# Storing a softmax's row reciprocals straight from their columns, one element at a time

## The chip, the cores and the metric

One core of one Trainium2 chip runs the whole program. The metric is the device time of one execution in microseconds (us), as the median of several runs.

## The reference

A decoder block on one sequence of 1024 tokens and 1024 channels, in float32. After a root-mean-square norm, one matrix product gives queries, keys and values for 8 attention heads of 64 channels, the two halves of a spatial gate, and one forget value per head and token. What matters here is the attention:

```python
c = jnp.cumsum(log_f, axis=1)
logits = jnp.einsum('bqhd,bkhd->bhqk', qi, k) * scale + ci[..., None] - c_k
p = jax.nn.softmax(jnp.where(causal, logits, -jnp.inf), axis=-1)
out = jnp.einsum('bhqk,bkhd->bqhd', p, v)
```

The attention's result and the gate's result are joined, multiplied by `w_out` and added to the input. A gated MLP with a short causal convolution and a last norm follow.

## The kernel before, in words

The stages are: input norm and products (to about 205 us in the profile), attention (to about 370), output product and second norm (to about 420), the MLP's up products (to about 840), the down products. Matrix operands are split into a high and a low part, and each product takes three matrix multiplications, so that float32 accuracy is kept. The attention stage is the one that the change touches.

**One head.** Head `h` has 8 blocks of 128 queries. `logits_mm` (L900) multiplies queries and keys into PSUM, block 7 first; `logits_min` (L910) masks on VectorE and finds each row's minimum; `logits_exp` (L927) takes the exponential on ScalarE in place and adds each row into column `j` of `rows[h]`, a tile of 128 rows by 8 blocks. `turn_p` (L935) turns blocks of the exponentials on TensorE (L946), ScalarE copies the high part (L947) and VectorE forms the low part (L948). `values` (L953) multiplies them with the values (L965) into a 64-by-1024 result `attF[p][.., 0, ..]`, with the 64 channels on partitions, two heads to a pair `p`. The result is not normalised there.

**The steps.** A head is five steps; 40 steps are walked by the loop at L1051. A step first turns what the next step needs, then multiplies its own values, and beside that starts the logits of head `h+1`. At step 1 of a head VectorE takes the reciprocals of its row sums (L1075), and `row_tail(h)` (L863) is called. It must bring the reciprocals, which lie as 128 partitions by 8 columns, into the order of the 1024 tokens, and repeat them on 64 partitions: the tile is turned on TensorE to 8 by 128 (L868), copied to SBUF by ScalarE (L869), stored to a 4 KB scratch `rsd[h]` in HBM by a DMA that ScalarE's queue issues (L870), and loaded back, repeated 64 times, into the second half of `attF[p]` by a DMA on SyncE's queue (L871), 256 KB.

**Who uses it.** `pair_half` (L874) multiplies result and reciprocals and splits the product. For pairs 0 to 2 it does so on GpSimd (L880 to L882), two halves of a pair, after its second head; for pair 3 on VectorE and ScalarE at the stage's end. GpSimd has other work in line behind it: in head 2 the low parts of the second half of the gate's output weights (`sg_split`, L716, its line L161), which the filler products need (below), and from head 5 on the attention's output weights (`wo_load`, L1003). The tile of `attF` is one of four buffers of the tag `H`, which the exponentials of odd heads use as well.

**Fillers.** Between the steps TensorE does pieces of another product, the gate's part of the output (`sg_out`, L978, matrix multiplications L990 to L992): one token block of 512 channels each, at steps 1 and 4 of heads 1 to 5, more in head 0. Each needs a load of the input `raw` (L986) on SyncE's queue, is added to it on VectorE (L993), and is stored (L994). `raw` tiles come from four buffers. `head_loads(h+2)` (L809, L813 to L821) brings queries and keys of a later head, about 1.3 MB, once a head.

**What sets the order.** A recording layer places the instructions of each engine in one line; engines run theirs in order and meet at semaphores. SyncE's queue too is one line: a DMA that waits holds up all DMAs behind it. DMAs take one of eight completion semaphores in turn, so a DMA also waits until the one eight places before it has landed. Matrix multiplications and turns of this stage are chained by `seq` (L696), so that their order on TensorE is fixed by the program. Elsewhere, at L391, the program stores 128-by-8 row scales into an 8-by-128 scratch `rbd` in HBM with the same kind of access pattern, once, and loads them back repeated (L392):

```python
act.dma_start(out=rbd.rearrange("a p -> p a"), in_=rstd1)
sp.dma_start(out=rb, in_=rbd.rearrange("a b -> (a b)").unsqueeze(0).to_broadcast((P, 1024)))
```

In the profile L391 shows under the line of a recording helper, L44.

Of the kernel before, what the change touches and what calls it, by code (L numbers as in the profile page):

```python
# [14 lines left out]
P = 128  # L15
# [44 lines left out]
def after(tc, later, earlier):  # L60
    tc.add_manual_dep(later.ins, earlier.ins.name, mybir.DependencyInfo(
        mybir.DependencyClass.NoSync, mybir.DependencyReason.DATA), reason="order")
# [3 lines left out]
def block_kernel(ctx: ExitStack, tc: tile.TileContext, xT, xtok, wuv, wv0, wv1, wqk, cpk, bfv,  # L66
                 ggain, g2r, gfr, wsp, woa, wos, wup, wdn, out):
    nc = tc.nc
    act, dve, pool, pe, sp = Line(nc.scalar, tc), Line(nc.vector, tc), Line(nc.gpsimd, tc), nc.tensor, nc.sync
# [13 lines left out]
    def nm(s):  # L83
        uid[0] += 1
        return f"{s}_{uid[0]}"
# [6 lines left out]
    def sb(tag, shape, dt=F32):  # L92
        return (raws if tag == "raw" else late if tag in LATE else early).tile(shape, dt, tag=tag, bufs=BUFS[tag], name=nm(tag))

    def bank():
        return psa.tile([P, 512], F32, tag="b", bufs=BB, name=nm("pb"))
# [28 lines left out]
    ident = cst.tile([P, P], F32, name="ident")  # L125
# [23 lines left out]
    rsd = drm.tile([8, 8, P], F32, name="rsd")  # L149
# [546 lines left out]
    def seq(m):  # L696

        if order:
            after(tc, m, order[0])
        order[:] = [m]  # L700
# [78 lines left out]
    idr = sb("t01", [P, 1024])  # L779
# [83 lines left out]
    def row_tail(h):  # L863

        p, hh, rs = h // 2, h % 2, rows[h]
        ptr = bank()
        rt = idr[0:8, 640 + P * hh:640 + P * (hh + 1)]
        seq(pe.transpose(ptr[0:8, 0:P], rs, ident))  # L868
        act.copy(rt, ptr[0:8, 0:P])  # L869
        act.dma_start(out=rsd[h], in_=rt)  # L870
        sp.dma_start(out=attF[p][hh * 64:hh * 64 + 64, 1, :],  # L871
                     in_=rsd[h].rearrange("a b -> (a b)").unsqueeze(0).to_broadcast((64, 1024)))

# [177 lines left out]
    for n, step in enumerate(STEPS):  # L1051
        h, s = n // 5, n % 5
# [24 lines left out]
        for c, (g, pt, js) in enumerate(zip(step, now, NEXT[s])):  # L1077
            out_copy = values(g, pt) or out_copy
            last_copy = out_copy
            if h < 7:  # L1080
                for j in js:
                    due.append((h + 1, j, logits_min(h + 1, j, logits_mm(h + 1, j, place()))))
            if s == (1 if h < 7 else 2) and c == (h == 7):
                row_tail(h)
# [594 lines left out]
```

## Time and profile before

| What | Value |
|---|---|
| Median of 3 runs | 1058.69 us (1058.6 to 1058.9) |
| The profiled execution, its own time | 1059.72 us |
| Its span in the trace | 1058.0 us |
| TensorE clock granted, mean | 0.999 |
| TensorE busy | 1046.3 us of the span |
| VectorE, ScalarE, GpSimd busy | 884.0, 571.1, 235.8 us |
| Turns of the row reciprocals (L868) | 8, first at 238.3 us, last at 367.0 us |

Times in the trace count from the start of the span. A row of the timeline gives the start, the duration, the engine, the line, the operation and its operands, and in brackets how long the engine had been idle and for whom it waited. "ACTq" and "SPq" are the queues of ScalarE and SyncE, where a DMA's row is the time of its issue and not of its transfer. Rows of windows give the busy time of each engine in a stretch, then the granted clock, the DMA engines' share and the GB/s that they moved. The prediction shows the rows that it uses.

### The profile page before, as it was taken

What the parts mean: (1) busy time and instruction counts of PE and PEld (TensorE: products, weight loads), DVE (VectorE), ACT (ScalarE), POOL (GpSimd) and SP (SyncE); (2) the same over time, 40 slices, a digit from 0 to 9 for tenths busy, and PEclk for the clock granted to TensorE, in tenths of its full rate; (3) what the DMA queues carried; (4) which work ended last, traced back from release to release, by engine and by line L of the source; (5) the groups of instructions that cost most, each with busy time, mean ns of one, the idle gap of its engine ahead of it and who ended that gap; (6) DMA issues with size and microseconds to landing.
All of it is one profiled execution on the core that took longest, in us unless ns stands there. A gap on an engine that the chain in (4) does not pass through costs nothing.

```text
span 1058.0 us, 14612 instructions
## 1 busy us (share of the span) xinstructions
PE 1046.3 (99%) x5156; PEld 880.3 (83%) x5156; DVE 884.0 (84%) x1297; ACT 571.1 (54%) x1013; POOL 235.8 (22%) x177
## 2 busy tenths in 40 slices
PE   9999999999999999999999999999999999999997
PEld 6988888988889888888888888888888888888885
DVE  6999787777778869998999989989897866897774
ACT  6776544456766746654444444444444544454653
POOL 0003241420420740154333323323321000000000
PEclk9999999999999999999999999999999999999999
DMA  9623466856555344222255322331322899333432
GB/s 323 219 8 134 129 162 167 224 153 190 168 163 170 122 174 173 72 89 100 80 170 179 120 96 94 120 122 59 132 96 80 302 328 314 102 99 100 146 119 94
DMA packets 67184, 155.78 MB, mean 147 GB/s; under 512 B 9028, under 2 KB 9748, under 8 KB 67112
## 3 DMA queue, kind: packets, MB, share of 16 engines
q1 hardware_dynamic: 65800, 154.82, 45.8%
q8 instruction: 40, 0.66, 0.3%
q14 instruction: 32, 0.26, 0.1%
q10 hardware_dynamic: 1312, 0.04, 0.1%
HBM read 111.96 MB, written 42.87 MB: 146 GB/s over the span
## 4 chain that ended last, share of the span: by engine, by line
PE 94%; DVE 2%; DMA 1%; ACT 1%; POOL 1%; issue 0%; SPq 0%; POOLq 0%; ACTq 0%; DVEq 0%
PE k L1529 20%; PE qc L1271 11%; PE qa L1271 11%; PE qd L1271 11%; PE ps L259 5%; PE qb L1271 5%; PE pb L259 5%; PE pb L965 3%; PE pb L946 3%; PE qa L417 2%; PE qc L417 2%; PE qd L417 2%; PE pl L906 2%; PE pl L907 2%; PE pf L990 1%; PE pf L992 1%
## 5 line engine op out<-in xcount | busy, mean ns | idle before, releaser
L1529 PE MATMUL k<-whb,wha 128*128 128x512 f32 x924 | 209.7, 389 | 0.0
L1529 PEld LDWEIGHTS k<-whb,wha 128*128 128x128 f32 x924 | 173.4, 188 | 36.2 <-DVE wha L161 0.2
L1271 PE MATMUL qc<-xT,whb 128*128 128x512 f32 x540 | 129.8, 389 | 0.2 <-ACT whb L155 0.2
L1271 PE MATMUL qa<-xB,wha 128*128 128x512 f32 x528 | 127.5, 390 | 0.0
L1271 PEld LDWEIGHTS qc<-xT,whb 128*128 128x128 f32 x540 | 101.3, 188 | 21.5 <-ACT whb L155 0.5
L1271 PEld LDWEIGHTS qa<-xB,wha 128*128 128x128 f32 x528 | 98.8, 188 | 20.9 <-DVE wha L161 0.4
L155 ACT CAST wha<-sg 128x512 fp32r<-128x512 f32 x77 | 47.8, 622 | 96.7 <-PE k L1529 86.4
L155 ACT CAST whb<-sg 128x512 fp32r<-128x512 f32 x82 | 50.5, 618 | 88.0 <-PE qc L1271 67.7
L161 DVE TENSOR_TENSOR wha<-sg,wha 128x512 fp32r<-128x512 f32 x77 | 52.7, 687 | 40.5 <-ACT wha L155 40.4
L947 ACT CAST pt<-pb 128x512 fp32r<-128x512 f32 (+1 forms) x80 | 42.2, 544 | 43.1 <-PE pb L946 34.2
L1271 PE MATMUL qd<-xB,whb 128*128 128x512 f32 x264 | 63.7, 389 | 0.0
L1271 PE MATMUL qd<-xT,whb 128*128 128x512 f32 x264 | 63.7, 389 | 0.0
L1155 POOL TENSOR_TENSOR sg<-raw 128x512 f32<-128x512 f32 x20 | 31.1, 1556 | 139.5 <-DVE whb L161 78.0
L1271 PE MATMUL qb<-xT,whb 128*128 128x512 f32 x252 | 61.0, 389 | 0.0
L161 DVE TENSOR_TENSOR whb<-sg,whb 128x512 fp32r<-128x512 f32 x82 | 57.0, 697 | 4.4 <-ACT whb L155 4.3
L948 DVE TENSOR_TENSOR pt<-pb,pt 128x512 fp32r<-128x512 f32 (+1 forms) x80 | 48.8, 634 | 12.3 <-ACT pt L947 11.0
L1271 PEld LDWEIGHTS qd<-xT,whb 128*128 128x128 f32 x264 | 49.5, 188 | 10.5 <-DVE u L1378 0.3
L1271 PEld LDWEIGHTS qd<-xB,whb 128*128 128x128 f32 x264 | 49.6, 188 | 10.3
L1271 PEld LDWEIGHTS qb<-xT,whb 128*128 128x128 f32 x252 | 47.2, 188 | 10.0 <-DVE whb L161 0.3
L965 PE MATMUL pb<-pt,V 128*128 128x256 f32 x320 | 52.1, 287 | 0.3 <-DVE pt L948 0.2
L1158 POOL TENSOR_TENSOR sg<-sg,raw 128x512 f32<-128x512 f32 x20 | 33.0, 1650 | 63.8 <-DVE whb L161 63.8
L965 PEld LDWEIGHTS pb<-pt,V 128*128 128x128 f32 x320 | 43.8, 190 | 2.6 <-DVE pt L948 0.4
(411 smaller groups left out, 2271.8 us busy)
## 6 DMA issues: line engine op xcount, KB each, us to landing
raw<-wup SPq DMA_DIRECT2D x44, 512.0 KB
sg<-hx SPq DMA_DIRECT2D x77, 256.0 KB
hx<-hs SPq DMA_DIRECT2D x44, 256.0 KB
hx<-ca SPq DMA_DIRECT2D x35, 256.0 KB
xT<-wdn SPq DMA_DIRECT2D x28, 256.0 KB
x<-kd SPq DMA_DIRECT2D x24, 256.0 KB
A<-xtok SPq DMA_DIRECT2D x8, 512.0 KB
raw<-wqk SPq DMA_DIRECT2D x8, 512.0 KB
```

The source lines that it names most:

```text
L155: act.copy(h, src)
L161: return eng.tensor_tensor(out=l, in0=src, in1=f32(h), op=ALU.subtract)
L259: pe.matmul(banks[m], xs(n, xi, k)[:, ms], w[:, wi, :], start=(first and k == 0 and c == 0 and (own or m % 2 == 0)), stop=(k == 3 and c == ...
L417: pe.matmul(ps, w[:, wi, ks], xs(n, xi, k), start=(first and c == 0), stop=(c == 11), skip_group_check=True)
L946: seq(pe.transpose(ptr[:, c:c + P], tj[jj][:, k * P:(k + 1) * P], ident))
L947: casts.append(act.copy(pt[:, 0, 0:w], ptr[:, 0:w]))
L948: los.append(dve.tensor_tensor(out=pt[:, 1, 0:w], in0=ptr[:, 0:w], in1=f32(pt[:, 0, 0:w]), op=ALU.subtract))
L965: seq(pe.matmul(po[0][:, oo:oo + n], lhs, pt[:, s, o:o + n], start=(k == 0 and s == 0), stop=(s == 1 and half)))
L1155: pool.tensor_tensor(out=s[0], in0=a21, in1=a22, op=ALU.add)
L1158: pool.tensor_tensor(out=s[3], in0=s[1], in1=a12, op=ALU.add)
L1271: pe.matmul(ps, w[:, wi, ks], xb[:, xi, k, :], start=(first and n == 0), stop=(n == 11), skip_group_check=True)
L1529: pe.matmul(banks[bk + m], xh[:, xi, ms], wh[:, wi, :], start=(first and p_ == 0 and n == 0), stop=(p_ == NP - 1 and n == 2), skip_group_c ...
```

## The change

For heads 0 to 6, `row_tail` no longer turns the reciprocals on TensorE and copies them. ScalarE's queue issues a DMA that reads the 128-by-8 tile as it lies and writes its elements to the places in `rsd[h]` at which the load L871 reads them. Head 7 keeps the turn, the copy and the store. The load back is the same. All lines below L865 stand 3 lines further down in the changed file; the text names the lines of the kernel before.

```diff
         p, hh, rs = h // 2, h % 2, rows[h]
-        ptr = bank()
-        rt = idr[0:8, 640 + P * hh:640 + P * (hh + 1)]
-        seq(pe.transpose(ptr[0:8, 0:P], rs, ident))
-        act.copy(rt, ptr[0:8, 0:P])
-        act.dma_start(out=rsd[h], in_=rt)
+        if h < 7:
+            act.dma_start(out=rsd[h].rearrange("a p -> p a"), in_=rs)
+        else:
+            ptr = bank()
+            rt = idr[0:8, 640 + P * hh:640 + P * (hh + 1)]
+            seq(pe.transpose(ptr[0:8, 0:P], rs, ident))
+            act.copy(rt, ptr[0:8, 0:P])
+            act.dma_start(out=rsd[h], in_=rt)
         sp.dma_start(out=attF[p][hh * 64:hh * 64 + 64, 1, :],
                      in_=rsd[h].rearrange("a b -> (a b)").unsqueeze(0).to_broadcast((64, 1024)))
```

## The prediction

> **What bounds the kernel now.** First the page: the engines' shares, then the chain that ended last. Then a table of windows over the middle of the attention stage, of which the sum row of 50 windows of 1 us (230 to 280 us) is shown.
>
> ```profile
> span 1058.0 us, 14612 instructions
> PE 1046.3 (99%) x5156; PEld 880.3 (83%) x5156; DVE 884.0 (84%) x1297; ACT 571.1 (54%) x1013; POOL 235.8 (22%) x177
> PE 94%; DVE 2%; DMA 1%; ACT 1%; POOL 1%; issue 0%; SPq 0%; POOLq 0%; ACTq 0%; DVEq 0%
> ...
> sum 50.00, PE 49.74 PEld 44.13 DVE 37.31 ACT 32.72 POOL 11.35; mean PE 0.99 PEld 0.88 DVE 0.75 ACT 0.65 POOL 0.23
> ```
>
> TensorE has work all the time, in the attention stage too (49.74 of 50 us). So only two things can move the end: TensorE work that goes, and a wait of TensorE that is new. All else has cover, and the question is how thick it is.
>
> **What goes.** Seven turns, seven copies. The rows of L868 and L869, from the views by line, and the turn of head 1 between its neighbours in TensorE's timeline:
>
> ```profile
> L868 PE MATMUL pb<-ident,rs x8: 270/272/274, 238.4 to 367.1; 128*8 128x128 f32 x8
> L868 PEldq EVENT_SEMAPHORE  x7: 51/51/51, 256.3 to 366.5; - x7
> L869 ACT COPY t<-pb x8: 237/238/254, 239.4 to 367.4; 8x128 f32<-8x128 f32 x8
> ...
> 257.26 0.27 PE L868 MATMUL pb<-ident,rs 128*8 128x128 f32 x1
> 257.29 0.65 PE L965 MATMUL pb<-pt,V 128*128 128x256 f32 x4
> ```
>
> A turn lasts 0.27 us, but the next matrix multiplication starts 0.03 us behind it: they are pipelined. With its semaphore (0.05 us) I take 0.03 + 0.05 = 0.08 us each, 7 x 0.08 = 0.6 us. The ends are 7 x 0.03 = 0.2 and 7 x 0.27 = 1.9 us; I stand near the lower, since the starts, not the durations, add up on a full engine. The copies, 7 x 0.24 = 1.7 us, are hidden: ScalarE is busy 32.72 of 50 us. Without that cover they would be 1.7 us of gain.
>
> **What is added: the store's own time.** The attention stage never shows such a store, but L391 is one: 128 x 8 elements of 4 bytes into the same kind of scratch, issued on the same queue. Its issue, the issue of the load that waits for it, the waits of SyncE's queue, and windows of 2 us:
>
> ```profile
> 67.83 0.38 ACTq L44 DMA_DIRECT2D rbd<-rstd  x1
> 77.95 0.33 SPq L392 DMA_DIRECT2D t<-rbd  x1
> SPq L392 <- DMA rbd<-rstd: 7.1, 1, 7.1
> SPq L871 <- DMA rsd<-t: 14.1, 6, 3.7
> ...
> 70.00 0.80 SPq L401 DMA_DIRECT2D G<-wv  x2
> 81.10 0.75 POOL L474 TENSOR_TENSOR G<-G 128x264 f32<-128x264 f32 x1 [79.38 <-DMA G<-wv]
> ...
> 70.00:72.00 2.00, 2.00 (x10) 1.65 (x10) 2.00 (x3) 0.62 (x1) 0.00 (x0) 1.00 1.39 15
> 72.00:74.00 2.00, 2.00 (x11) 1.65 (x10) 2.00 (x4) 0.62 (x1) 0.00 (x0) 1.00 0.14 13
> 76.00:78.00 2.00, 2.00 (x11) 1.65 (x10) 2.00 (x4) 2.00 (x5) 0.00 (x0) 1.00 0.75 20
> 82.00:84.00 2.00, 2.00 (x11) 1.65 (x10) 2.00 (x3) 0.09 (x1) 0.75 (x1) 1.00 1.03 401
> ```
>
> From issue to landing 77.95 - 67.83 = 10.1 us, of which SyncE's queue waited 7.1. The rearranged store of today costs that queue 14.1 us in six waits, 2.4 each. And it is not only late: loads issued at 70.00 moved at 13 to 20 GB/s (last column) until the store was done, and the first was usable at 81.10; at 82 the same queue runs at 401. So a store is a **blackout** of about 10 us for all transfers. Seven of them are 70 us in a stage of 155.
>
> The Trainium skill, "DMA: Bandwidth & Descriptors", section "Anatomy of one DMA", fits a transfer's time as about 2.0 us plus its bytes over 436 GB/s, from transfers that GpSimd issued. By it the 4 KB take an estimated 2.0 us, L871 would be issued about as early as today, and the sum would hold the gain alone. The trace's 10.1 us disagrees, which is why this stands below only as a rival.
>
> Under load the store can be shorter by nothing that I see, and longer: at L391 the queue was empty when it was issued. At head 1's store loads are still running (windows of 1 us):
>
> ```profile
> 256.00:257.00 1.00, 1.00 (x9) 0.91 (x8) 0.84 (x4) 0.73 (x2) 0.00 (x0) 1.00 1.04 221
> 257.00:258.00 1.00, 1.00 (x9) 0.91 (x8) 0.83 (x3) 1.00 (x2) 0.00 (x0) 1.00 0.53 107
> ```
>
> 221 + 107 = 328 KB still to move, some 0.9 us at 370 GB/s. I take 10.1 + 0.9 = 11.0 us, with 10 as the lower end and 15 as the upper (half as long again).
>
> **What is moved.** The order of the changed program differs from before on few places, all in this stage. On ScalarE the store stands earlier, between the two casts (L947) that follow the reciprocal, not behind the next exponential. On SyncE L871 moves by one to two places and the filler loads L986 of heads 1 to 4 now stand behind it. Other DMAs keep their order. So what is queued behind the waiting L871 is: filler loads, filler stores, the next `head_loads`, the output weights.
>
> On ScalarE the store's issue (0.38 us) sits ahead of a cast, and in head 2 it waits for the reciprocal (276.01 to 276.21 below) where the cast began at 275.66: 276.21 + 0.38 - 275.66 = 0.9 us late. That cast is used by TensorE a step later, over 3 us; cost nothing, 0.9 us without that cover.
>
> ```profile
> 255.78 0.59 ACT L947 CAST pt<-pb 128x512 fp32r<-128x512 f32 x1 [0.56 <-PE pb L946]
> 275.66 0.59 ACT L947 CAST pt<-pb 128x512 fp32r<-128x512 f32 x1 [0.22 <-PE pb L965]
> 256.04 0.20 DVE L1075 RECIPROCAL rs<-rs 128x8 f32<-128x8 f32 x1
> 276.01 0.20 DVE L1075 RECIPROCAL rs<-rs 128x8 f32<-128x8 f32 x1
> ```
>
> **The waits, head by head.** Stores go out at about 256.4 (head 1: the cast's end, 255.78 + 0.59) and 276.3 (head 2). With 11.0 us L871 goes at 267.4 and 287.3, where it went at 260.48 and 279.15. Its 256 KB then take 2.5 us at least (issued at 260.48, moved by 263 in the windows) and 5.1 at most (head 7: 369.62 to 374.69, with other loads ahead); I take 3.0. The first who could be late:
>
> ```profile
> 260.48 0.45 SPq L871 DMA_DIRECT2D H<-rsd  x1
> 279.15 0.45 SPq L871 DMA_DIRECT2D H<-rsd  x1
> 262.00:263.00 1.00, 1.00 (x9) 0.91 (x8) 0.54 (x2) 0.99 (x2) 0.00 (x0) 1.00 0.92 277
> 369.62 0.45 SPq L871 DMA_DIRECT2D H<-rsd  x1
> 374.69 1.29 DVE L884 TENSOR_TENSOR H<-H 128x512 f32<-128x512 f32 x2 [3.11 <-DMA H<-rsd]
> ...
> 266.86 1.28 POOL L880 TENSOR_TENSOR H<-H 128x512 f32<-128x512 f32 x1 [48.47 <-DVE H L974]
> 272.65 5.05 POOL L161 TENSOR_TENSOR whl<-raw,whl 128x512 fp32r<-128x512 f32 x4
> 279.21 0.39 PE L991 MATMUL pf<-whl,G 128*128 128x512 f32 x1
> 290.59 0.69 DVE L993 TENSOR_TENSOR raw<-pf,raw 128x512 f32<-128x512 f32 x1 [0.84 <-issue]
> ```
>
> *GpSimd, pair 0.* L880 starts at 267.4 + 3.0 = 270.4, not 266.86. Behind it in line stand, unchanged, the rest of the pair and the four low parts of the gate's weights. Today GpSimd also idles 0.5 us in that row; from 270.4 it runs through, and the four end at 280.6, not 277.7. The fourth is needed by TensorE's L991 at 279.21: a **hole of 1.4 us** on the full engine. At a store of 10.1 us it is 0.5, at 12 it is 2.4: it grows one to one.
>
> *Filler loads.* Behind head 2's L871 stands the load for the filler added at 290.59: issued at 287.8, in at about 291.3 (3.5 us, behind L871's bytes). VectorE has about 1.2 us until TensorE feels it, and the hole above moves all of this by 1.4. Nothing, until the store takes some 11.5 us. The one behind head 1's (added at 271.57) has a microsecond more. All others are needed 9 us or more after their new issue.
>
> *`head_loads`, output weights, other pairs.* Needed about 18 us after they can start; the blackout takes 11. GpSimd's pair 2 and weight splits end some 2 us later, at 367, before the output product takes them. Nothing; with a store of 15 us here too little is left.
>
> **The sum.** -0.6 + 1.4 = +0.8 us on the profiled execution's 1059.72 (span 1058.0 and 1.7 around it). The median of the runs is 1.0 below that execution, so +0.8 on 1058.69: **1059.5 us**.
>
> **The rivals.**
>
> *The store is much longer under load: slower.* For it: 13 to 20 GB/s for what shares the engines, and at heads 0 to 3 the queue is not empty. Against: the queue at 70 us was backed up during most of that store as well, and it still took 10.1. The mechanism is the hole of pair 0 with the late filler load of head 2 added. It decides from 11.7 us of store on, where the sum passes +2.1. At 14 us: 1.4 + 3.0 = 4.4 for the hole; the filler load in at 276.3 + 14 + 0.5 + 3.5 = 294.3 against 290.59 + 1.2, 2.5 us; less 0.6: +6.3, **1065.0 us**. At 15 us 1067. The Trainium skill, same page, section "Latency and other measured facts", puts HBM access at 0.2 us on average and 2 us at high load. By that the busier attention stage would lengthen every element's write, this rival's direction; no row here shows such a store under load.
>
> *The store is short: a small gain.* If L391's 10.1 us are its place and not its kind, L871 goes about as today, and only TensorE's gain stays: 1058.69 - 0.6 = **1058.1 us**, at most 1.9 less. For it: the six stores of today land in 2.4 us. Against: these write 8 rows of 512 bytes.
>
> **How the numbers follow.** A difference under 0.2%, 2.1 us, can't be told from no change here. Forecast (store of 10 to 11.7 us) 0.44, all within 0.2%; long store 0.45, slower; short store 0.11, of which 0.03 is over 0.2% faster (more bounded by the turns than their 0.27 us). Faster 0.03, same 0.44 + 0.08 = 0.52, slower 0.45. The likeliest case alone reaches from 1058.1 to 1060.8. The range of eight in ten, from the short store (1058.1, less half a microsecond for how far its gain is known) to one of 15 us: 1057.6 to 1067.
>
> **What would show it.** After: SyncE waits 9 to 11 us before each L871 of heads 0 to 6; GB/s near 20 behind each store; the first L880 near 270 us and a wait of TensorE for L161's weights near 279. Wrong if the waits stay near 2.4 us (short store), or if VectorE waits for `raw` at L993 or TensorE for `head_loads` (long store). A loss spread over all heads would mean that contention, not the one hole, is the price.

## The result, and the profile after

The changed kernel is slower: 1076.98 us in the median (1066.47 to 1080.38, 6 runs) against 1058.86 (1058.60 to 1059.05) for the kernel before on the same chip, ratio 1.0154 with a 95% interval of 1.0127 to 1.0181. The prediction was 1059.5 us, its range 1057.6 to 1067. In four later measurements the unaltered changed kernel gave 1063.7 to 1065.1 us, so two things are to be explained: some 5 to 6.5 us over the kernel before on the same chip that came back each time, and the rest of the first measurement. The profiled execution is the 1066.47 us one, so the traces show the first part and not the second. The text below names lines of the changed file; the rows of dead_late, pool_order and head1_twice bear the line numbers of those files, which differ by a few.

The page of the changed kernel: span, engines, the DMA queue that holds the stores (packets, MB, share of time; before it had 1312 packets), and the shares of the chain that ended last.

```profile
span 1064.7 us, 14585 instructions
PE 1047.6 (98%) x5149; PEld 880.1 (83%) x5149; DVE 885.6 (83%) x1297; ACT 571.1 (54%) x1006; POOL 237.4 (22%) x177
...
q10 hardware_dynamic: 8480, 0.04, 0.5%
...
PE 82%; DVE 7%; DMA 6%; ACT 2%; issue 2%; POOL 1%; SPq 1%; ACTq 0%; POOLq 0%; DVEq 0%
```

The queue has 7168 packets more, 7 x 1024, for the same bytes: one for each element. DMA was 1% of the chain and is 6%. The waits of SyncE's queue and of TensorE (the latter from 205 to 420 us), each with its sum, count and longest:

```profile
SPq L874 <- DMA rsd<-rs: 52.5, 6, 10.8
```

```profile
PE pf L994 <- POOL whl L161: 2.7, 4, 1.9
PE pl L910 <- DMA x<-kd: 1.7, 1, 1.7
PE ps L1219 <- DVE xn L1201: 1.4, 2, 0.8
```

SyncE's wait for the reciprocals has grown from 14.1 to 52.5 us (six waits in both), and TensorE has three waits that the kernel before did not have. Where they lie, the windows show: TensorE is the first number after the comma.

```profile
...
275.00:280.00 5.00, 3.07 (x17) 2.18 (x16) 3.39 (x7) 1.91 (x4) 4.94 (x5) 1.00 1.07 264
280.00:285.00 5.00, 4.28 (x22) 3.08 (x23) 1.25 (x2) 0.80 (x2) 3.85 (x4) 1.00 1.25 71
350.00:355.00 5.00, 3.30 (x22) 2.74 (x21) 2.13 (x6) 2.06 (x8) 0.03 (x1) 1.00 0.97 257
395.00:400.00 5.00, 4.21 (x24) 3.32 (x22) 4.96 (x7) 2.16 (x7) 4.92 (x4) 1.00 0.79 311
400.00:405.00 5.00, 4.34 (x24) 3.35 (x23) 4.80 (x7) 3.85 (x8) 2.40 (x2) 1.00 0.68 211
sum 30.00, PE 24.03 PEld 18.73 DVE 18.93 ACT 15.62 POOL 18.57; mean PE 4.00 PEld 3.12 DVE 3.16 ACT 2.60 POOL 3.10
```

The kernel before, in the same windows:

```profile
sum 30.00, PE 29.98 PEld 25.92 DVE 24.31 ACT 21.47 POOL 13.36; mean PE 5.00 PEld 4.32 DVE 4.05 ACT 3.58 POOL 2.23
```

29.98 - 24.03 = 5.95 us of idle TensorE (the sums hold 270 to 275 us as well), of the 6.7 by which the span grew (1058.0 to 1064.7), in three places and not spread over the heads. The first is the hole that the prediction named. The chain from 250 to 300 us (start, duration, what):

```profile
255.81 12.93 DMA rsd<-rs
268.76 3.51 DMA H<-rsd
272.43 1.29 POOL H L883
273.78 0.62 POOL A L884
...
277.63 4.99 POOL whl L161 x4
282.67 0.50 PE pf L994
```

Head 1's store takes 12.93 us, its load back 3.51, and GpSimd starts pair 0 at 272.43; the gate's weights come behind it and TensorE waits for each. The second hole is new to the prediction. The timeline around head 5's store (issues on ScalarE's and SyncE's queues, and TensorE's wait in brackets):

```profile
335.44 0.41 ACTq L867 DMA_DIRECT2D rsd<-rs  x1
335.47 0.98 SPq L813 DMA_DIRECT2D x<-qd  x1
...
342.21 0.25 SPq L821 DMA_DIRECT2D x<-ncd  x1
349.22 0.44 SPq L874 DMA_DIRECT2D H<-rsd  x1
353.78 0.48 PE L910 MATMUL pl<-x,x 66*128 66x512 f32 x1 [1.70 <-DMA x<-kd]
```

And the last of the same loads before:

```profile
330.60 0.45 SPq L821 DMA_DIRECT2D x<-ncd  x1
```

`head_loads` for head 7, whose last issue was at 330.60, now waits on SyncE's queue until head 4's store is in (L874 at 329.51) and a filler's store behind it (3.2 us more), and so goes out at 335.47 to 342.21, into head 5's store (335.44 to 349.22): both are late. This **piling up** turned out to be the heart of the matter. The third hole, at 395 to 405 us, stands behind the last pair and the second norm.

### The profile page after: what moved, and what is told of

The parts are those of the page before. It is cut to its first block, busy times and chain, and to the rows that moved or that the text cites. A ratio compares the mean times of both kernels' runs of the same rounds, so it can differ in the third digit from the quotient of the medians.

```text
span 1064.7 us, 14585 instructions
## 1 busy us (share of the span) xinstructions
PE 1047.6 (98%) x5149; PEld 880.1 (83%) x5149; DVE 885.6 (83%) x1297; ACT 571.1 (54%) x1006; POOL 237.4 (22%) x177
## 4 chain that ended last, share of the span: by engine, by line
PE 82%; DVE 7%; DMA 6%; ACT 2%; issue 2%; POOL 1%; SPq 1%; ACTq 0%; POOLq 0%; DVEq 0%
PE k L1532 20%; PE qc L1274 11%; PE qa L1274 11%; PE qd L1274 11%; PE qb L1274 5%; PE pb L968 2%; PE qa L417 2%; PE ps L259 2%; PE pb L949 2%; PE qc L417 2%; PE qd L417 2%; DMA x<-kd 1%; PE pl L909 1%; DMA rsd<-rs 1%; PE pl L910 1%
## 5 line engine op out<-in xcount | busy, mean ns | idle before, releaser
L161 DVE TENSOR_TENSOR wha<-sg,wha 128x512 fp32r<-128x512 f32 x77 | 53.0, 690 | 39.7 <-ACT wha L155 39.6
L161 DVE TENSOR_TENSOR whb<-sg,whb 128x512 fp32r<-128x512 f32 x82 | 57.1, 698 | 4.4 <-ACT whb L155 4.3
L1274 PEld LDWEIGHTS qb<-xT,whb 128*128 128x128 f32 x252 | 47.2, 188 | 10.1 <-DVE whb L161 0.3
```

Source lines behind the costliest of these rows:

```text
L161: return eng.tensor_tensor(out=l, in0=src, in1=f32(h), op=ALU.subtract)
L1274: pe.matmul(ps, w[:, wi, ks], xb[:, xi, k, :], start=(first and n == 0), stop=(n == 11), skip_group_check=True)
```

## The experiments

Theories: **W**, the waits: only the late load back counts, by the holes behind it. **B**, the blackout: what the stores do to all other transfers counts, even if nobody waits for the stores. Two more were formed on the way: **P**, piling up: a store is long because loads are under way, and holds back loads that are then under way at the next one. **C**, the clock: a TensorE wait makes the granted clock fall, and costs more than itself. "Store" below is the time from its issue to the issue of the load that needs it. For head 6 this is not the store's length: SyncE's queue stands there for GpSimd and for filler stores, and in the kernel before, too, the load goes 8.4 us after (353.18 to 361.62). So only heads 0 to 5 are counted.

**The changed kernel again.**

> The changed kernel once more, unaltered. Two theories of its loss. Theory W (wait): a store takes 11 to 14 us here instead of 10, SyncE's queue stands still behind it, and TensorE loses time only where a follower has no slack: the low parts of the gate's weights on GpSimd (2.8 us near 280 in the first trace of it) and the loads of head 7 (1.7 us near 352). Theory C (clock): the executions that took 1072 to 1080 us show a granted clock of 0.991 to 0.994 where the first shows 0.999; at 1050 us of TensorE work 0.7% is 7 us, so most of what separates them from 1066 is a slower TensorE and not a longer wait. W expects 1066 to 1080 with all of the loss in TensorE's waits; C expects that a trace at clock 0.992 has windows with a clock under 1 after the waits, and the same matrix multiplication takes longer there.

1063.73 us (1062.77 to 1065.91), ratio 1.0050 [1.0035, 1.0065]. Stores of 10.6 to 13.3 us. The excess over 1066 did not come back.

**Four heads by elements, and head 1 alone.**

```diff
-        if h < 7:
+        if h in (0, 2, 3, 4):        # four_heads
+        if h == 1:                   # head1
```

> The store by elements for heads 0, 2, 3 and 4 alone; heads 1, 5 and 6 keep the turn and the copy. W: none of these four has a follower without slack, so 1058 to 1060 us, although four of seven stores are there. A rival, theory B (blackout): each store slows all transfers and costs its share wherever it stands; four sevenths of 8 to 18 us, so 1063 to 1069.

> The store by elements for head 1 alone. W: the hole of pair 0 on GpSimd comes back whole, TensorE waits 2 to 4 us near 280 for the gate's weights, and the time is 1061 to 1063 us (with C up to 8 more, if one wait is enough to lower the clock). B: one seventh of 8 to 18 us, 1060 to 1061.5, with no wait of TensorE that stands out.

four_heads: 1058.70 us (1057.91 to 1059.57), ratio 0.9999 [0.9990, 1.0009], with stores of 13.1, 8.0, 11.0 and 12.4 us and no new wait of TensorE over 0.4. So these four long stores cost nothing that can be told, since those behind them have time. head1: 1059.26 (1058.55 to 1060.28), ratio 1.0005 [0.9995, 1.0014], no hole: a miss. Its store was short (timeline):

```profile
254.76 0.39 ACTq L867 DMA_DIRECT2D rsd<-rs  x1
...
262.62 0.45 SPq L874 DMA_DIRECT2D H<-rsd  x1
```

7.9 us alone, 12.9 as one of seven. The store's length is not its own; P was formed here.

**Stores that nobody waits for.** The kernel before, with a second, element-wise store of each reciprocal tile into a scratch that is never read, some 8 us later (the line that makes the scratch `rsx` is left out here and below):

```diff
+        if s == 3 and h < 7:
+            after(tc, act.dma_start(out=rsx[h].rearrange("a p -> p a"), in_=rows[h]), casts[-1])
```

> The kernel before with its turns, copies and stores kept, and for heads 0 to 6 a second store by elements into a scratch that nobody reads, issued about 8 us after the first, when the load L871 has been issued. So all seven blackouts are there and nobody waits for their end. W: the repeated load and with it GpSimd's pair come as before; only transfers that are under way are late, 1059 to 1062 us. B: as slow as the changed kernel, 1066 or more.

1070.48 us (1068.10 to 1074.63), ratio 1.0115 [1.0091, 1.0139]. W alone falls: a store costs without a load that reads it. The view of SyncE's waits:

```profile
SPq L987 <- DMA hpd<-raw: 51.5, 8, 10.7
```

A filler's store and the next issue on SyncE's queue, with two of the windows between them (the last column is GB/s):

```profile
245.40 0.33 SPq L995 DMA_DIRECT2D hpd<-raw  x1
256.43 0.33 SPq L987 DMA_DIRECT2D raw<-xtok  x1
...
250.00:252.00 2.00, 2.00 (x10) 1.63 (x9) 1.46 (x5) 1.59 (x5) 0.00 (x0) 1.00 0.14 0
254.00:256.00 2.00, 2.00 (x18) 1.95 (x17) 1.86 (x5) 1.42 (x5) 0.00 (x0) 1.00 0.00 0
```

And the chain from 250 to 300 us:

```profile
258.76 6.80 DMA hpd<-raw
265.62 0.35 SPq L987
266.07 6.20 DMA H<-rsd
272.50 1.30 POOL H L881
```

Head 0's unread store goes out at 245.75. The filler's store issued just ahead of it holds SyncE's queue until 256.43, 11.0 us, where the same store took 3.4 in the kernel before (245.78 to 249.13). What is behind it comes late and together: head 1's step sends its loads from 256.81 to 261.0, and the next filler's store takes 6.80 us among them, not in a blackout but at 230 to 344 GB/s. The load back goes at 266.07 instead of 260.48, into head 1's unread store (266.69), and takes 6.20 us, 3.51 in the changed kernel. GpSimd starts at 272.50, as in the changed kernel. So B holds too, and the price is paid by whichever transfer falls into the blackout or stands behind one that does. At the stage's end it is ScalarE: it issues head 7's store only at 377.26, behind a load of output weights that took 12.45 us beside head 6's unread store (363.75), and TensorE waits 2.7 us. The seven stores also shift which DMA waits for which completion semaphore, so the 11.7 us are no bare price of seven blackouts.

**Heads 0 and 1, and heads 4 to 6.** P says that the store of head 1 becomes long if head 0 has one.

> The store by elements for heads 0 and 1 alone. Head 1 alone cost 0.5 us at most, its store took 7.9 us and no wait of TensorE followed; in the changed kernel the same store took 11 to 13. Theory P (piling up): head 0's store holds back the loads behind it, so they are under way when head 1's store comes, and lengthen it. P expects head 1's store at 10.5 to 13 us again, the hole near 280 back, 1061 to 1063 us. If stores do not touch each other: 8 us, 1059 to 1060.

> Element by element for heads 4, 5 and 6 alone, three stores in a row, none before. If stores pile up wherever they follow each other, those of heads 5 and 6 take 11 us and more and head 7's loads are late near 350 us: 1060 to 1064. If only the first heads, with the filler's loads and GpSimd's pair 0 behind them, have no slack, it is the time of before within 1 us, although the stores are as long.

heads01: 1062.79 us (1061.34 to 1066.12), ratio 1.0042 [1.0026, 1.0058]. Its timeline:

```profile
255.31 0.37 ACTq L867 DMA_DIRECT2D rsd<-rs  x1
...
267.92 0.44 SPq L874 DMA_DIRECT2D H<-rsd  x1
```

12.6 us instead of 7.9, by head 0's store alone, and TensorE waits 2.0 us for L161's weights. The loads of head 1's step went out from 248.18 to 253.83 in head1, ahead of the store, and go from 253.63 to 258.09 here, into it: P holds, and two heads make over half of the steady loss (a fall of the clock included, last section). heads456: 1059.19 us (1057.75 to 1060.53), ratio 1.0006 [0.9997, 1.0016], with stores of 8.6 and 11.9 us for heads 4 and 5. Head 5's is longer there too, but three in a row do not yet make `head_loads` late for TensorE.

**Head 1 with two stores**, an unread one ahead on the same queue:

```diff
+        if h == 1:
+            act.dma_start(out=rsx[h].rearrange("a p -> p a"), in_=rs)
+            act.dma_start(out=rsd[h].rearrange("a p -> p a"), in_=rs)
```

> The store by elements for head 1 alone, with a second one of the same size into an unread scratch ahead of it on the same queue. W: the store that is waited for lands about 8 us later (15 to 16 us from the first issue), the pair on GpSimd starts that much later, and TensorE waits 4 to 7 us near 280 for the gate's weights; with the clock falling behind so long a wait, 1064 to 1069 us. If the wait of GpSimd were not the way in which the store costs, the time would stay near head 1's 1059.3.

1066.17 us (1065.48 to 1067.35), ratio 1.0072 [1.0055, 1.0089]. The load back goes 16.5 us after the first issue. The time is as expected, but by luck: the filler load behind the load back is the late one, and TensorE waits only 0.5 us for the gate's weights, not 4 to 7. TensorE's waits:

```profile
PE pb L951 <- DVE raw L998: 4.0, 1, 4.0
```

**The first hole alone removed.** GpSimd does the gate's weights ahead of pair 0:

```diff
-            pool.tensor_tensor(out=f[:, 0, o], in0=f[:, 0, o], in1=f[:, 1, o], op=ALU.mult)
+            x = pool.tensor_tensor(out=f[:, 0, o], in0=f[:, 0, o], in1=f[:, 1, o], op=ALU.mult)
+            if p == 0:
+                after(tc, x, splits[0])
```

> The changed kernel with one order turned round on GpSimd: the low parts of the gate's weights ahead of pair 0 instead of behind it. All stores stay as they are. W: TensorE no longer waits for those weights near 280; 2 to 3 us come back, more if that wait had lowered the clock. The waits at the end of attention stay. B (each store has a fixed price): no change against the changed kernel.

> The changed kernel a third time, as the measure for the three beside it. Its executions have taken 1063 to 1080 us. W with the clock: what differs between executions is how long the stores take (10.6 to 14.0 us so far) and whether one of the waits grows past some 3 us, where the granted clock falls to 0.5 for about 3.4 us (seen once, in the kernel with late stores). Expected: again a store in flight when the next head's loads are issued, holes of 2 to 3 us near 280, and the more below 0.999 the mean clock, the longer the execution, about 10 us for each 0.010.

pool_order: 1064.48 us (1060.22 to 1067.43), ratio 1.0052 [1.0031, 1.0073]; the changed kernel beside it: 1065.12 (1062.83 to 1070.13), 1.0068 [1.0041, 1.0095]. The hole at 275 to 285 us is gone, TensorE is full there. But pool_order's waits of TensorE are now:

```profile
PE pl L912 <- DMA x<-kd: 4.0, 2, 3.0
PE ps L1221 <- DVE xn L1203: 1.9, 2, 1.2
```

What one hole gives back is lost at the next late transfer: the intervals overlap, no gain can be told. A TensorE that isn't held up at 280 us arrives earlier at what comes next, and `head_loads` comes when the queues let it.

**The clock.** In again2 a TensorE wait of 2.8 us for `head_loads` is followed by this (windows of 1 us; the clock stands after the five engines):

```profile
354.00:355.00 1.00, 0.00 (x0) 0.00 (x0) 0.00 (x0) 0.08 (x1) 0.00 (x0) 1.00 1.06 201
355.00:356.00 1.00, 0.02 (x1) 0.05 (x1) 0.00 (x0) 0.00 (x0) 0.00 (x0) 0.77 0.97 205
356.00:357.00 1.00, 1.00 (x3) 0.81 (x4) 0.00 (x0) 0.00 (x0) 0.00 (x0) 0.50 0.98 307
...
362.00:363.00 1.00, 1.00 (x9) 1.00 (x8) 0.81 (x2) 0.77 (x2) 1.00 (x3) 0.81 0.97 194
```

The clock is at half from about 355.5 to 362.4. To try C without any store by elements, the kernel before was given ten (gap_short) or twenty-two (gap_long) small copies on ScalarE in head 3 and a turn on TensorE that waits for the last:

```diff
+        if h == 3 and s == 2:
+            for _ in range(10):
+                x = act.copy(pad[:, 8:16], rows[h])
+                after(tc, x, casts[-1])
+            seq(pe.transpose(bank()[0:8, 0:P], pad[:, 8:16], ident))
```

> The kernel before, with no element store anywhere; at head 3, step 2, ScalarE is given ten extra copies of 128 x 8 elements (some 0.2 us each) behind that step's last cast, and TensorE one extra turn of 8 columns that waits for the last of them. It makes one TensorE gap of some 1 to 2.5 us without any change to the DMA traffic. If the gap alone makes the granted clock fall (clock theory), rows of 0.5 follow it for about 3.4 us in the profile, or in some executions, and the time is the gap plus up to 1.7 us: 1060 to 1063. If the clock falls only with the stores' traffic, the clock stays at 1.00 and the time is before plus the gap alone: 1059.5 to 1061.

> The same with twenty-two copies: one gap of some 4 to 5 us. Clock theory: rows of 0.5 for about 3.4 us behind the gap in the profile in every execution, 1064 to 1066. Without it: the gap alone, 1062.5 to 1064. If the fall depends on where a gap lies and not on its length, the short one may show it and this one not.

gap_short: a wait of 1.9 us, 1061.75 us (1060.95 to 1062.64), ratio 1.0027 [1.0015, 1.0039]; in its profile (1060.96 us) the clock stays at 1.00. Of its other executions, three had a mean clock of 0.997 and took 1062.08 to 1062.64 us, two 0.998 and 0.999 with 1060.95 and 1061.42: falls in some of them would fit, but none of these was traced. gap_long: a wait of 4.6 us, 1065.53 us (1064.66 to 1065.77), ratio 1.0061 [1.0044, 1.0078], so 6.7 us for 4.6, at 0.996 or 0.997 in all four executions. Its windows:

```profile
303.00:304.00 1.00, 0.00 (x0) 0.00 (x0) 0.00 (x0) 0.84 (x6) 0.00 (x0) 0.88 0.08 31
304.00:305.00 1.00, 0.00 (x0) 0.00 (x0) 0.00 (x0) 0.88 (x5) 0.00 (x0) 0.50 0.00 0
...
310.00:311.00 1.00, 1.00 (x8) 0.90 (x7) 1.00 (x3) 0.98 (x4) 1.00 (x1) 0.71 0.00 0
```

The gap alone does it, with the DMA queues nearly empty: C holds for the long gap. The Trainium skill, "TensorE: Matmul & The Clock Gate", section "Part 1: The HAM clock gate (the "warmup" mystery)", says that the clock goes to half after an idle window of about 3.4 us, that the window runs freely, and that warming takes as long. The trace agrees in the half and in the steps: half-clock stretches were 3.4 us or 6.8 us. It differs in the gap needed (last section).

**Is 1077 us the chip's or the execution's?**

> The changed kernel, unaltered, once more on whichever chip it falls to, to see whether the 1077 us of the first measurement belong to the chip or to the execution. If the place and number of the falls of the granted clock differ from execution to execution, the time lies between 1063 and 1080 and each execution's time goes with its mean clock, about 1 us for each 0.001 of clock. If it belongs to the chip, this is again 1063 to 1066 or again near 1077, with little between.

> The changed kernel, unaltered, on whichever chip it falls to, with more executions. If the 1072 to 1080 us of the first measurement are executions in which the clock falls behind more of the waits, some of these show a mean clock of 0.994 or less and 1070 us or more; if they belong to the first chip alone, all lie between 1061 and 1070 us, as the twelve on three other chips did.

again3: 1064.84 us (1061.49 to 1065.81), ratio 1.0055 [1.0038, 1.0073]; again4: 1063.94 (1061.90 to 1064.15), ratio 1.0043 [1.0030, 1.0057]. None of the 17 later executions (on three chips) was above 1070.13 us. The time varied by 8.6 us between them, with mean clocks of 0.995 to 0.999, but the clock does not order them well. That of the first measurement did: 0.999 at 1066.47 us, 0.994 at 1072.51, 0.991 and 0.992 at 1076.28 to 1080.38. A mean clock 0.007 lower is 1065 x 0.007 = 7.5 us, an estimate, of the 10 to 14 us above the profiled execution. More falls of the clock fit that, but no trace of such an execution exists, and the measurement did not come back. That it belongs to that chip alone, as again4's expectation has it for this outcome, is not settled either: no later run is known to have been on the chip of the first measurement. **What made it 1077 stays open.**

No version beat the kernel before: four_heads is level with it.

## Why the prediction was wrong

**The failed step: "I take 10.1 + 0.9 = 11.0 us".** The stores of heads 0 to 5 took 11.3 to 14.1 us in the changed kernel's profile, head 1's 12.9. L391's 10.1 us was no bare price to which a backlog is added, since head 1 alone took 7.9 with traffic ahead of it. And the backlog was mis-sized: I read it from the trace before, 0.9 us, while the change makes its own, by loads that the previous store holds back (7.9 to 12.6 us by one more store). The sum treated the stores as seven separate ones. That, with the step on `head_loads` below and the stage's end, makes up the part that came back (2.7 + 1.7 + 1.4 = 5.8 us of waits in the profile): the profiled execution and the medians of all four later measurements lie within the stated range. The first measurement's 1076.98 us lies above it, and which step failed there stays open.

**The hole: right in place and mechanism.** Predicted were GpSimd's start at 270.4, with L161's weights late behind it, and a hole that grows one to one: 1.4 us at 11.0 and so 3.3 at 12.9. Measured were 272.4 and 2.7 us of waits.

**"`head_loads`, output weights, other pairs. [...] Nothing": wrong.** The premise was "Needed about 18 us after they can start; the blackout takes 11". But `head_loads` starts later too, behind L874 on SyncE's queue, into the next store (and head 5's took 13.8 us, near the 15 at which the prediction saw too little left). It cost 1.7 us in the profile, 4.1 in again2, 1.1 in again3, 4.0 in pool_order and nothing in again and again4. The end of the stage lost 1.4 more; that it comes from the late last pair was read from the trace and not tried by itself.

**The filler loads: nearly nothing, as said up to 11.5 us of store.** They cost 0.2 us in the profile, 1.1 in again3, and 4.0 at 16.5 us (head1_twice). The rival named them as its second loss, at 14 us, where in fact it was `head_loads`.

**The rival "much longer under load"** was the right case: 1065.0 us at 14 us of store, against 1066.47 in the profiled execution and medians of 1063.7 to 1065.1 in the later measurements. Its chance was put at 0.45, level with the forecast's 0.44. Its number is in part luck: it adds the filler's 2.5 us to the hole's 4.4, though the hole, as the prediction says itself, moves the filler's turn along (290.59 + 1.2 + 4.4 = 296.2 against 294.3). Without them it gives 1062.5 us; `head_loads` and the stage's end took their place. And by its own terms the sum passes +2.1 us at 11.9 us of store (2.3 + 0.4 - 0.6), not at 11.7. I argued against it with L391, whose queue had been backed up too; the reading that was missing is what is queued behind seven in a row.

**Blackout:** seen, priced wrongly. The last column of the changed kernel's windows in head 0:

```profile
237.00:239.00 2.00, 2.00 (x17) 1.91 (x16) 1.61 (x3) 1.67 (x3) 0.00 (x0) 1.00 1.29 117
239.00:241.00 2.00, 2.00 (x18) 1.91 (x16) 1.74 (x4) 1.62 (x5) 0.00 (x0) 1.00 0.93 40
241.00:243.00 2.00, 2.00 (x11) 1.68 (x11) 2.00 (x5) 0.57 (x2) 0.00 (x0) 1.00 0.45 14
243.00:245.00 2.00, 2.00 (x14) 1.70 (x12) 0.42 (x1) 0.03 (x1) 0.00 (x0) 1.00 0.13 8
```

117 to 8 GB/s, as called for; but SyncE's queue issues nothing here from 236.88 to 246.05, so the last rows show an empty queue as well. That transfers under way are held up is shown by dead_late (11.0 us for 3.4). The prediction charged the blackout only through L871; dead_late shows that it costs as much through other transfers. At L391, too, the 13 to 20 GB/s shown are not all: from 74 to 76 us 44 were moved.

**The clock** was no term of the sum. Where it falls, a wait of 2 to 3 us costs up to 1.7 or 3.4 us more (half of 3.4 or 6.8 us).

**The gain, -0.6 us:** neither shown nor refuted. four_heads, with four turns less and no new wait, stands between 1.1 us below and 1.0 above the kernel before.

## What to carry to other kernels

A store by elements is priced by what stands around it and not by its bytes: 4 KB took 8 us with little around it and 9.5 to 14.2 in the changed kernel's traces, and transfers that ran beside it were held up. Before a change lengthens a DMA that comes round once a loop, lay out one whole period of the queue with all times moved, loads included, and ask whether the delay is gone before the next one starts; if not, it adds up. A saving of some tenths of a microsecond on a full engine is lost in a single wait, and removing one hole brought nothing here that can be told, as the next late transfer took its place (pool_order).

## What the runs showed of the hardware

**The clock falls after short gaps, in some executions.** Falls stood behind TensorE waits of 4.0 us (head1_twice), 2.8 (again2), 2.7 (dead_late) and 1.7 (heads01 and again4); the waits of 1.9 us in the changed kernel's profile and in gap_short had none, and pool_order's of 3.0 us had none either (windows in its wait and behind it):

```profile
331.00:332.00 1.00, 0.00 (x0) 0.00 (x0) 0.00 (x0) 0.00 (x0) 0.00 (x0) 1.00 0.95 188
333.00:334.00 1.00, 1.00 (x11) 1.00 (x10) 0.92 (x1) 0.00 (x0) 0.00 (x0) 1.00 0.17 51
```

heads01, windows behind its wait, from 278.1 us on with TensorE partly idle:

```profile
279.00:280.00 1.00, 0.72 (x3) 0.57 (x3) 0.00 (x0) 0.00 (x0) 1.00 (x2) 0.66 1.04 325
280.00:281.00 1.00, 1.00 (x4) 0.70 (x3) 0.00 (x0) 0.00 (x0) 1.00 (x2) 0.50 0.97 198
281.00:282.00 1.00, 1.00 (x3) 0.65 (x3) 0.00 (x0) 0.00 (x0) 1.00 (x2) 0.50 0.48 123
282.00:283.00 1.00, 1.00 (x5) 0.78 (x5) 0.00 (x0) 0.00 (x0) 0.98 (x1) 0.63 0.68 205
```

At half clock for (1 - 0.66)/0.5 + 1 + 1 + (1 - 0.63)/0.5 = 3.4 us, although TensorE's own wait was 1.7 us. In again2 and gap_long the same sum gives 6.8 us. The length of a wait alone does not decide: again and again4 are the same kernel, TensorE idles 2.0 us from 275 to 280 us in both, and only in again4 does the clock fall (to 0.50 from 280 to 282 us). The same section of the Trainium skill has the window run freely; by that the same gap could have a fall in one execution and none in another, as it has here. That this is the reason is argued and not shown. What share of idle in a window is enough is open.

**A store's length depends on its neighbours.** Head 1's took 7.9 us alone, 12.6 behind head 0's, 12.9 among seven; in heads456 those of heads 4 and 5 took 8.6 and 11.9. The length goes with how shortly before the store the loads of `head_loads` (L813) began, in the 45 stores of heads 0 to 5 of ten traces (the changed kernel's five, pool_order, four_heads, head1, heads01, heads456): 7.9 to 8.6 us of store where they began 6.6 to 6.8 us before it, 9.5 to 10.6 at 3.7 to 4.9, and 10.4 to 14.2 at 3.5 or less. No store ahead is needed: head 0's, with none ahead and the loads 2.8 us before it, took 14.1 us in the changed kernel and 12.8 to 13.6 in its four later traces.
